# Score products of the gated levels: the moving operand cut from all 128 tokens of a chunk to the 64 that query

## The chip, the cores and the metric

The kernel runs on one NeuronCore of a Trainium2 chip, in one launch. The metric is the device time of that launch in microseconds (us), lower is better. In the profile PE is the matrix engine (TensorE) that streams a moving operand through stationary weights, PEld is the same engine's weight loads, DVE is VectorE, ACT is ScalarE, POOL is GpSimd, and SP is the engine whose queue issues the DMAs.

## The reference, cut to what matters

One layer of a hybrid decoder runs over a prompt of 2048 tokens and over 8 samples of 8 tokens, all float32. The layer has four retention heads and four gated heads (HGRN2) side by side, then an output projection and a squared-ReLU MLP.

```python
# gated heads: f = lb + (1 - lb) * sigmoid(x W_f), k = 1 - f, log_g = log f, dk = dv = 128
b = jnp.cumsum(gb, axis=2)                                   # within a chunk, per key dimension
diff = b[:, :, :, None, :] - b[:, :, None, :, :]
decay = jnp.exp(jnp.where(causal[:, :, None], diff, -jnp.inf))
A = jnp.einsum('bhtd,bhsd,bhtsd->bhts', qb, kb, decay)       # score of query t with key s
o = jnp.einsum('bhts,bhsv->bhtv', A, vb) + jnp.einsum('bhtd,bhdv->bhtv', qb * jnp.exp(b), S)
S_new = S * jnp.exp(b_last)[..., None] + jnp.einsum('bhsd,bhsv->bhdv', kb * jnp.exp(b_last - b), vb)
```

The score matrix `A` of a gated head has a decay for each of the 128 key dimensions, so it is not one matrix product. The change lies in how the kernel makes `A`.

## The kernel before, in words

**Groups and heads.** The 2112 tokens are three groups with 640, 768 and 704 columns (`GROUPS`); the last holds the 64 sample tokens ahead of 640 prompt tokens. A group's prompt tokens are chunks of 128: 5, 6 and 5 of them, 16 in all. `mix` goes through the heads p = 0 to 3 of a group. For each it issues six projections, a value product (L744 to L751) and, interleaved with these, the score and state work of one retention and one gated head. After the three groups come the MLPs, which end the program and which the change does not touch.

**Operands.** The projections run as split float32: weights and activations are each a rounded part and a remainder (`hi`, `lo`), and `proj` (L344) issues three products for each block and half of the columns, 320, 384 or 352 columns at a time. Score products run in plain float32 straight from the slabs, `[128, 768]` tiles of SBUF. The profile shows each of these as two matmul instructions, each with a weight load of its own.

**Levels of a gated head.** The 128x128 scores of a chunk are made level by level. At level w the chunk falls into blocks of 2w tokens. With the log decay measured from the middle of a block, `decayed` (L908, L909) fills a slab `qk`: keys times decay in the first half of each block, queries times decay in the second half. One product over the 128 key dimensions then gives the scores of all pairs (key in a first half, query in the second half of the same block). The levels are w = 64, 32, 16, 8, 4 and 2:

- 64 and 32 are made by `corners` (L978): one matmul for each block, w columns of weights and w moving columns.
- 16, 8 and 4 (blocks of 32 to 8 tokens) are made by `kept`: one matmul for each chunk with the whole `qk` of the chunk as both weights and moving operand (L921), then one masked copy for each half of the group's chunks (`copy_predicated`, L922). It moves into the score tile `AT` what the mask `msk[:, i]` selects. That mask is nonzero only for a key in a first half and a query in the second half of the same block.
- 2 is made by column sums over products (`quad`, L512, L513, L1010). The diagonal and the neighbouring pairs go the same way (`own`, L942; `next_to`, L965).

For the sample tokens, level 4 alone has `kept` with sg = 2: one 128x128 product (L915) and a masked copy into `ATs` (L916).

**Order of the work.** `at`, `later` and `tick` form an agenda: one tick passes with each block of projection matmuls, and the work of a head falls due so many ticks after its start. What each engine finally does in which order is decided when the program is built: a scheduler places the instructions by an estimate of their durations, except for those held by `keep_in_program_order`. An engine runs its own list in order and waits on semaphores for the others.

**Names used below.** `mm` are PSUM tiles of 512 columns from a pool of four, `po` those in which a head's outputs add up (L1101 and L1103; L784 and L787 for the samples), `AT`/`ATs` the gated scores, `qm` the sample queries that POOL copies (L780), `ret_s` and `hg_s` the sample states that SP loads (L772).

Of the kernel before, what the change touches and what calls it, by code (L numbers as in the profile page):

```python
# [15 lines left out]
P = 128  # L16
# [5 lines left out]
NS = NSEQ * SLEN  # L22
# [11 lines left out]
LEVELS = (64, 32, 16, 8, 4, 2)  # L34
NLV = len(LEVELS) + 2
# [167 lines left out]
class Kernel:  # L203
# [659 lines left out]
    def mixer(self, g, p, b, t0):  # L863


        nc, T, n0 = self.nc, g.T, g.ns
        con, msk = self.con, self.msk
        n = g.n // C
        q, k, f = b["q"], b["k"], b["f"]
        rq, rk = b["rq"], b["rk"]  # L870
        cols = [slice(n0 + C * c, n0 + C * (c + 1)) for c in range(n)]
# [38 lines left out]

        def kept(i, qk, sg):

            if sg == 2:
                ps = self.mm(P)
                nc.tensor.matmul(ps, qk[:, :P], qk[:, :P], start=True, stop=True)  # L915
                nc.vector.copy_predicated(self.ATs, msk[:, NLV + i], ps)  # L916
                return
            seg, m = g.segs[sg], len(g.segs[sg])
            ps = self.mm(m * P)
            for j, c in enumerate(seg):  # L920
                nc.tensor.matmul(ps[:, j * P:(j + 1) * P], qk[:, cols[c]], qk[:, cols[c]], start=True, stop=True)  # L921
            nc.vector.copy_predicated(self.AT[sg][:, :m], msk[:, i].unsqueeze(1).to_broadcast([P, m, P]),  # L922
                                      ps.rearrange("p (c t) -> p c t", t=P))


        def own_products():
# [86 lines left out]
        def level(i, sg):  # L1013
            w = LEVELS[i]
            if w == 2:
                quad(sg)
            elif w >= 32:
                corners(w, sg)
            else:
                kept(i, x["qk", w], sg)  # L1020
# [113 lines left out]
        for i, w in enumerate(LEVELS):  # L1134
            t = 6 + step * i
# [12 lines left out]
        t = 6 + step * len(LEVELS)  # L1148
# [680 lines left out]
```

## Time and profile before

| | |
|---|---|
| median of 3 runs | 2497.9 us (2497.9 to 2498.38) |
| profiled execution, own time | 2499.3 us |
| its span | 2497.5 us |
| PE busy / PEld busy | 2483.4 / 2465.2 us |
| DVE / ACT / POOL busy | 1883.1 / 1246.5 / 371.2 us |
| granted PE clock | 0.999 |
| L921, PE busy | 54.4 us, 384 instructions |
| L922, DVE busy | 39.0 us, 72 instructions |

The span runs from the first to the last instruction of the core; the execution's own time is 1.8 us more. A busy time is a union: where two matmuls overlap in the records, the time is counted once. The duration in a row for one matmul or weight load is from its start to its end, and several are under way at a time, so what one costs a full PE is the distance from its start to the next one's start, not its duration. The mixing stage with the levels lies between about 50 and 1120 us.

### The profile page before, as it was taken

What the parts mean: (1) busy time and instruction counts of PE and PEld (TensorE: products, weight loads), DVE (VectorE), ACT (ScalarE), POOL (GpSimd) and SP (SyncE); (2) the same over time, 40 slices, a digit from 0 to 9 for tenths busy, and PEclk for the clock granted to TensorE, in tenths of its full rate; (3) what the DMA queues carried; (4) which work ended last, traced back from release to release, by engine and by line L of the source; (5) the groups of instructions that cost most, each with busy time, mean ns of one, the idle gap of its engine ahead of it and who ended that gap; (6) DMA issues with size and microseconds to landing.
All of it is one profiled execution on the core that took longest, in us unless ns stands there. A gap on an engine that the chain in (4) does not pass through costs nothing.

```text
span 2497.5 us, 41452 instructions
## 1 busy us (share of the span) xinstructions
PE 2483.4 (99%) x16536; PEld 2465.2 (99%) x16536; DVE 1883.1 (75%) x2453; ACT 1246.5 (50%) x1674; POOL 371.2 (15%) x312
## 2 busy tenths in 40 slices
PE   9999999999999999999999999999999999999998
PEld 9999999999999999999999999999999999999998
DVE  7666866667685766686875899776699878778987
ACT  6665653444464444453644554544454436445544
POOL 5223304324411442340000000000000000000000
PEclk9999999999999999999999999999999999999999
DMA  7454575465566665868866856576675545867552
GB/s 264 170 183 172 206 252 180 161 228 186 189 205 244 216 217 197 265 210 257 283 222 214 284 196 214 176 237 222 201 264 177 188 151 192 282 195 246 195 188 89
DMA packets 191655, 525.67 MB, mean 210 GB/s; under 512 B 20963, under 2 KB 62435, under 8 KB 191462
## 3 DMA queue, kind: packets, MB, share of 16 engines
q1 hardware_dynamic: 191318, 523.01, 61.9%
q8 instruction: 130, 2.13, 0.3%
q14 instruction: 63, 0.52, 0.1%
q10 hardware_dynamic: 144, 0.02, 0.0%
HBM read 389.51 MB, written 132.39 MB: 209 GB/s over the span
## 4 chain that ended last, share of the span: by engine, by line
PE 97%; DVE 1%; ACT 1%; DMA 0%; issue 0%; SPq 0%; DVEq 0%; ACTq 0%
PE pj L344 29%; PE pf L1212 26%; PE pj L1212 25%; PE pjv L751 8%; PE mm L921 2%; PE po L1101 1%; PE mm L1109 1%; PE po L1103 1%; PE mm L978 1%; PE mm L513 1%; PE mm L512 1%; PE mm L1035 1%; PE mm L853 1%; PE po L787 1%; DMA slab<-x 0%
## 5 line engine op out<-in xcount | busy, mean ns | idle before, releaser
L273 ACT CAST hi<-raw 128x1024 fp32r<-128x1024 f32 x392 | 411.8, 1050 | 612.7 <-PE pf L1212 258.0
L344 PE MATMUL pj<-slab,hi 128*128 128x320 f32 (+2 forms) x3072 | 660.7, 328 | 2.9 <-DVE slab L650 1.3
L1212 PE MATMUL pf<-slab,hi 128*128 128x320 f32 (+2 forms) x2768 | 658.4, 321 | 0.0
L1212 PE MATMUL pj<-slab,hi 128*128 128x352 f32 (+2 forms) x2608 | 621.3, 322 | 0.0
L287 DVE TENSOR_TENSOR lo<-raw,hi 128x1024 fp32r<-128x1024 f32 x392 | 486.2, 1241 | 113.2 <-ACT hi L273 107.8
L344 PEld LDWEIGHTS pj<-slab,hi 128*128 128x128 f32 x3072 | 508.2, 188 | 5.7 <-DVE slab L650 1.6
L1212 PEld LDWEIGHTS pf<-slab,hi 128*128 128x128 f32 x2768 | 481.2, 188 | 0.0
L1212 PEld LDWEIGHTS pj<-slab,hi 128*128 128x128 f32 x2608 | 453.7, 188 | 0.1
L1212 PE MATMUL pf<-slab,lo 128*128 128x320 f32 (+2 forms) x1384 | 444.7, 321 | 0.0
L1212 PE MATMUL pj<-slab,lo 128*128 128x352 f32 (+2 forms) x1304 | 419.5, 322 | 0.0
L344 PE MATMUL pj<-slab,lo 128*128 128x320 f32 (+2 forms) x1536 | 379.0, 328 | 0.6 <-DVE lo L287 0.6
L344 PEld LDWEIGHTS pj<-slab,lo 128*128 128x128 f32 x1536 | 263.3, 188 | 1.5 <-DVE lo L287 1.1
L1212 PEld LDWEIGHTS pf<-slab,lo 128*128 128x128 f32 x1384 | 259.6, 188 | 0.0
L1212 PEld LDWEIGHTS pj<-slab,lo 128*128 128x128 f32 x1304 | 244.6, 188 | 0.0
L751 PE MATMUL pjv<-hi,slab 128*128 128x256 f32 (+1 forms) x1056 | 199.4, 285 | 0.0
L1303 ACT CAST slab<-slab 128x640 fp32r<-128x640 f32 (+2 forms) x192 | 145.4, 778 | 64.2 <-DVE slab L1314 51.7
L1307 DVE TENSOR_TENSOR slab<-slab 128x640 fp32r<-128x640 f32 (+2 forms) x192 | 167.3, 887 | 8.5 <-PE pj L1212 2.8
L751 PEld LDWEIGHTS pjv<-hi,slab 128*128 128x128 f32 (+1 forms) x1056 | 166.3, 190 | 1.4
L751 PE MATMUL pjv<-lo,slab 128*128 128x256 f32 (+1 forms) x528 | 149.2, 283 | 0.0
L902 ACT ACTIVATE slab<-slab 128x640 f32<-128x640 f32 (+2 forms) x72 | 56.3, 782 | 154.2 <-POOL slab L898 154.0
L751 PEld LDWEIGHTS pjv<-lo,slab 128*128 128x128 f32 (+1 forms) x528 | 100.3, 190 | 0.0
L1557 DVE TENSOR_TENSOR slab<-pf,slab 128x640 f32<-128x640 f32 (+2 forms) x88 | 77.7, 888 | 29.5 <-PE pf L1212 29.1
(222 smaller groups left out, 3012.4 us busy)
## 6 DMA issues: line engine op xcount, KB each, us to landing
raw<-w SPq DMA_DIRECT2D x264, 512.0 KB, 4.2
slab<-u SPq DMA_DIRECT2D x32, 384.0 KB, 4.6
u<-ld SPq DMA_DIRECT2D x30, 384.0 KB, 4.5
slab<-u SPq DMA_DIRECT2D x32, 352.0 KB, 4.5
u<-ld SPq DMA_DIRECT2D x30, 352.0 KB, 3.7
slab<-u SPq DMA_DIRECT2D x32, 320.0 KB, 5.0
u<-ld SPq DMA_DIRECT2D x30, 320.0 KB, 4.0
ld<-x SPq DMA_DIRECT2D x16, 384.0 KB, 3.8
```

What stands on the lines that cost most here:

```text
L273: self.nc.scalar.copy(hi, raw)
L287: self.nc.vector.tensor_tensor(out=lo, in0=self.second.pop(j), in1=hi.bitcast(F32), op=ALU.subtract)
L344: self.nc.tensor.matmul(pj[:, i, :T2], w, a[:, c0:c1], start=j == 0 and q == 0, stop=j == n - 1 and q == 2)
L512: self.nc.tensor.matmul(ps, self.ones_r, hi, start=True, stop=False)
L513: self.nc.tensor.matmul(ps, self.ones_r, lo, start=False, stop=True)
L751: nc.tensor.matmul(pj[:m, i * 256:(i + 1) * 256], a[:, s:s + m], ww, start=kb == 0 and q == 0, stop=m == C and kb == KB - 1 and q == 2, sk ...
L902: nc.scalar.activation(x["dd", w][:, a:T], x["dd", w][:, a:T], AF.Exp)
L921: nc.tensor.matmul(ps[:, j * P:(j + 1) * P], qk[:, cols[c]], qk[:, cols[c]], start=True, stop=True)
L1212: self.nc.tensor.matmul(*a, **k)
L1303: self.nc.scalar.copy(hi[:, :g.T], B[name][:, :g.T])
L1307: self.nc.vector.tensor_tensor(out=lo[:, :g.T], in0=B[name][:, :g.T], in1=hi.bitcast(F32)[:, :g.T], op=ALU.subtract)
L1557: nc.vector.tensor_tensor(out=r, in0=ps, in1=r, op=ALU.add)
```

## The change

In `kept` the moving operand is cut to the second halves of the blocks. The view `second` takes, of 128 columns, the w columns of the second half of each block: 64 columns, in runs of w = 16, 8 or 4 float32 values. The weights stay the whole chunk. The PSUM tile, the target in `AT` and the mask are cut to the same columns, so a masked copy goes over 64 columns of each chunk where it went over 128. For the samples the moving operand is the 32 columns of second halves among the 64 sample tokens, and the copy goes over these 32.

```diff
         def kept(i, qk, sg):
 
+            w = LEVELS[i]
+            second = lambda t: t.rearrange("p (n h m) -> p n h m", h=2, m=w)[:, :, 1]
             if sg == 2:
-                ps = self.mm(P)
-                nc.tensor.matmul(ps, qk[:, :P], qk[:, :P], start=True, stop=True)
-                nc.vector.copy_predicated(self.ATs, msk[:, NLV + i], ps)
+                ps = self.mm(NS // 2).rearrange("p (n m) -> p n m", m=w)
+                nc.tensor.matmul(ps, qk[:, :P], second(qk[:, :NS]), start=True, stop=True)
+                nc.vector.copy_predicated(second(self.ATs[:, :NS]), second(msk[:, NLV + i, :NS]), ps)
                 return
             seg, m = g.segs[sg], len(g.segs[sg])
-            ps = self.mm(m * P)
+            ps = self.mm(m * P // 2).rearrange("p (c n m) -> p c n m", c=m, m=w)
             for j, c in enumerate(seg):
-                nc.tensor.matmul(ps[:, j * P:(j + 1) * P], qk[:, cols[c]], qk[:, cols[c]], start=True, stop=True)
-            nc.vector.copy_predicated(self.AT[sg][:, :m], msk[:, i].unsqueeze(1).to_broadcast([P, m, P]),
-                                      ps.rearrange("p (c t) -> p c t", t=P))
+                nc.tensor.matmul(ps[:, j], qk[:, cols[c]], second(qk[:, cols[c]]), start=True, stop=True)
+            nc.vector.copy_predicated(self.AT[sg][:, :m].rearrange("p c (n h m) -> p c n h m", h=2, m=w)[:, :, :, 1],
+                                      second(msk[:, i]).unsqueeze(1).to_broadcast([P, m, P // (2 * w), w]), ps)
```

The scheduler places a few instructions differently because of it. Lines behind `kept` stand two lines further down in the changed kernel (L921 is L923, L922 is L924).

On PE the first place is the sample part of group 2, here head 1. L784 and L787 are the sample outputs, L810 the transposes of the sample keys, L838 the sample state products, L344 the projections around them. Before:

```order
L853 MATMUL mm<-con,slab 128x128 x3
L344 MATMUL pj<-slab,hi 128x352 x4
L344 MATMUL pj<-slab,lo 128x352 x2
L784 MATMUL po<-slab 128x128
L787 MATMUL po<-slab,ld 128x128 x8
L344 MATMUL pj<-slab,hi 128x352 x4
L344 MATMUL pj<-slab,lo 128x352 x2
L344 MATMUL pj<-slab,hi 128x352 x4
L344 MATMUL pj<-slab,lo 128x352 x2
L344 MATMUL pj<-slab,hi 128x352 x2
L810 MATMUL mm<-con,slab 96x128 x2
L838 MATMUL mm<-slab 128x512 x2
```

The same place on PE in the changed kernel:

```order
L853 MATMUL mm<-con,slab 128x128 x3
L344 MATMUL pj<-slab,hi 128x352 x2
L784 MATMUL po<-slab 128x128
L787 MATMUL po<-slab,ld 128x128 x8
L344 MATMUL pj<-slab,hi 128x352 x2
L344 MATMUL pj<-slab,lo 128x352 x2
L344 MATMUL pj<-slab,hi 128x352 x4
L344 MATMUL pj<-slab,lo 128x352 x2
L344 MATMUL pj<-slab,hi 128x352 x4
L344 MATMUL pj<-slab,lo 128x352 x2
L344 MATMUL pj<-slab,hi 128x352 x4
L810 MATMUL mm<-con,slab 96x128 x2
```

The retention samples' outputs (L784, L787) come four projection matmuls earlier, and the key transposes (L810) two later; L838 still follows L810 directly, and the gated samples' outputs, behind these rows, keep their distance of seven projection matmuls from L810.

On SP, in the same head, the loads around the sample states of the retention head; `w17hi` and `w17lo` are stored parts of a weight block. Before:

```order
L796 DMA ld<-slab 32x256 x2
L772 DMA ld<-ret_s 128x4x128
L256 DMA hi<-w17hi 128x1024
L256 DMA lo<-w17lo 128x1024
L772 DMA ld<-ret_s 128x4x128
```

And in the changed kernel:

```order
L796 DMA ld<-slab 32x256 x2
L256 DMA hi<-w17hi 128x1024
L256 DMA lo<-w17lo 128x1024
L772 DMA ld<-ret_s 128x4x128 x2
L1251 DMA sd11S_10121<-raw 128x1024
```

The first of the two state loads now stands behind the two weight loads.

On DVE, in head 0 of group 0, the masked copies of levels 8 and 4 between other work; L908 and L909 fill the `qk` slab of level 2, AT_173 and AT_174 are the two halves of `AT`. Before:

```order
L922 COPY_PREDICATED AT_173<-msk,mm 128x256
L908 TENSOR_TENSOR slab<-slab 128x160x2
L909 TENSOR_TENSOR slab<-slab 128x160x2
L922 COPY_PREDICATED AT_174<-msk,mm 128x384
L989 TENSOR_TENSOR slab<-slab 128x640
```

And in the changed kernel:

```order
L924 COPY_PREDICATED AT_173<-msk,mm 128x16x8
L908 TENSOR_TENSOR slab<-slab 128x160x2
L924 COPY_PREDICATED AT_174<-msk,mm 128x24x8
L909 TENSOR_TENSOR slab<-slab 128x160x2
L991 TENSOR_TENSOR slab<-slab 128x640
```

The second masked copy of level 8 has moved ahead of L909. Elsewhere PE shows differences of the same kind in head 3 of group 0 (column sums L512 and L513 up to eight projection matmuls later, outputs and states by one to four) and in head 3 of group 2. The products of `corners` and of `kept` keep their places in all heads, and POOL's list is unchanged.

## Prediction

> **What bounds the kernel now.** I read the page's busy times and its chain first, to see which engine sets the end; then what PE waits for; then, by line, the instructions that the change touches; then PE's two record streams in order of time, to see what one of these instructions costs.
>
> The page's span, its busy times, and the chain that ended last by engine:
>
> ```profile
> span 2497.5 us, 41452 instructions
> PE 2483.4 (99%) x16536; PEld 2465.2 (99%) x16536; DVE 1883.1 (75%) x2453; ACT 1246.5 (50%) x1674; POOL 371.2 (15%) x312
> PE 97%; DVE 1%; ACT 1%; DMA 0%; issue 0%; SPq 0%; DVEq 0%; ACTq 0%
> ```
>
> PE is the bound: 97% of the chain, and all but 14.1 us of the 2497.5 us span busy. So a microsecond off PE's stream is a microsecond off the time, and one off another engine is worth only what PE waits for it. The waits of PE come to seven rows, 5.6 us in all; the first and the last:
>
> ```profile
> PE pj L344 <- DVE slab L650: 1.3, 1, 1.3
> ...
> PE po L784 <- DVE slab L814: 0.2, 1, 0.2
> ```
>
> No row is of L921 or of a product that reads AT. But PE and PEld are both busy 99%, and this is one engine with two streams, loads of weights and matmuls. Which of the two sets the pace decides what fewer moving columns are worth. The products of the levels, by line and form:
>
> ```profile
> L921 PE MATMUL mm<-slab 128*128 128x128 f32 x384 | 54.4, 274 | 0.0
> L921 PEld LDWEIGHTS mm<-slab 128*128 128x128 f32 x384 | 51.9, 191 | 0.1
> L915 PE MATMUL mm<-slab 128*128 128x128 f32 x8 | 1.5, 272 | 0.0
> L978 PE MATMUL mm<-slab 128*64 128x64 f32 x128 | 12.6, 231 | 0.0
> L978 PEld LDWEIGHTS mm<-slab 128*64 128x64 f32 x128 | 9.2, 137 | 3.4 <-issue 0.8
> L978 PEld LDWEIGHTS mm<-slab 128*32 128x32 f32 x256 | 9.9, 112 | 5.3 <-issue 3.5 <-PE mm L1027 0.9 <-ACT slab L351 0.6
> ```
>
> 16 chunks, 4 heads, 3 levels and 2 instructions for each product make the 384, with 8 for the samples: 392 passes are touched. The mean time of one load goes 112, 137, 191 ns for 32, 64 and 128 columns of weights: some 0.8 ns for each column on top of a fixed part of some 87 ns. The weights keep their 128 columns.
>
> **What one pass costs.** The weight loads in order of time (start, length, count), at a run of four and at a run of six loads of L921, each up to the next load of a projection:
>
> ```profile
> 288.40 0.56 PEld L921 LDWEIGHTS mm<-slab 128*128 128x128 f32 x4
> 288.88 0.59 PEld L344 LDWEIGHTS pj<-slab,hi 128*128 128x128 f32 x4
> ...
> 216.16 0.78 PEld L921 LDWEIGHTS mm<-slab 128*128 128x128 f32 x6
> 216.86 0.19 PEld L344 LDWEIGHTS pj<-slab,hi 128*128 128x128 f32 x1
> ```
>
> Four loads take 0.48 us from start to start and six 0.70 us; the two more cost 0.22 us, so a pass costs 0.11 us. Load and matmul both have 128 columns here, and the two views cannot say which of them takes the 0.11. This place can, where the array has just been emptied, behind blocks of level 64 (L978, loads of 64 columns):
>
> ```profile
> 409.20 0.42 PEld L978 LDWEIGHTS mm<-slab 128*64 128x64 f32 x6
> 409.69 0.19 PEld L751 LDWEIGHTS pjv<-hi,slab 128*128 128x128 f32 x1
> 409.80 0.19 PEld L751 LDWEIGHTS pjv<-lo,slab 128*128 128x128 f32 x1
> ...
> 409.69 0.39 PE L751 MATMUL pjv<-hi,slab 128*128 128x256 f32 x1
> ```
>
> The matmul at 409.69 has nothing ahead of it but its own weight load, which starts with it. The next load starts when the first set of weights has gone into use, 0.11 us later. No earlier matmul can be what that load waits for: a load of 128 columns by itself takes the 0.11 us. And the six 64-column loads take (0.42 - 0.137)/5 = 0.057 us each from start to start, half of it, with 64 moving columns. So load and matmul cost alike per column, the load of one pass runs beside the matmul of the pass before, and the longer of the two is paid.
>
> The Trainium skill bears on this in its page "TensorE: Matmul & The Clock Gate", section "LDWEIGHTS (loading the stationary operand)", and speaks against the change: a load takes its columns of weights divided by 1.2 in ns, whatever the rows. By that rule, as an estimate, 128 columns take 107 ns and a pass could not fall below that. The emptied array's 0.11 us agrees.
>
> **The change part by part.**
>
> *The 392 passes.* Each matmul would take about 0.057 us by itself instead of 0.11, but the load of the next pass (128 columns, 0.11 us) still stands between it and the next matmul. A run of m chunks paid 2m times 0.11 us; afterwards it pays 2m loads of 0.11 us, and the projection's load behind the run also takes 0.11. What is late next is the weight load, at once. I take 0 us. The views resolve 10 ns, so the difference of six and four loads is good to 5 ns a pass; that bounds a gain, 392 x 0.005 = 2.0 us. The moving operand is now read in runs of 16, 8 or 4 values with equal gaps; no matmul of before does that. The nearest rows are DVE's masked copies, with contiguous and with every-second-column targets:
>
> ```profile
> L922 DVE COPY_PREDICATED AT<-msk,mm 128x384 f32<-128x384 uint8 x48 | 28.6, 595 | 15.1 <-PE mm L921 8.9 <-issue 4.0 <-ACT slab L902 1.6
> L922 DVE COPY_PREDICATED AT<-msk,mm 128x256 f32<-128x256 uint8 x24 | 10.6, 443 | 7.1 <-PE mm L921 3.4 <-ACT slab L902 1.8 <-issue 1.8
> L1010 DVE COPY_PREDICATED AT<-msk,mm 128x64 f32<-128x64 uint8 x128 | 22.8, 325 | 10.7 <-PE mm L513 10.7
> L965 DVE COPY_PREDICATED AT<-msk,mm 128x192 f32<-128x192 uint8 x16 | 9.3, 633 | 3.2 <-PE mm L513 3.2
> ```
>
> Contiguous, one more column costs (595 - 443)/128 = 1.2 ns; with a step of two, (633 - 325)/128 = 2.4 ns, twice as much. If PE's reading slowed by the same factor, a pass would stream 2 x 0.057 = 0.114 us, 4 ns over the load: 392 x 0.004 = 1.6 us slower. So this term is 0, from -2.0 to +1.6 us. The place in the array (rows, columns of weights) stays, so no array has to be emptied that was not.
>
> *The 72 masked copies.* They go over 128 or 192 columns instead of 256 or 384. At the contiguous price the 24 small ones cost 443 - 128 x 1.2 = 289 ns and the 48 large ones 595 - 192 x 1.2 = 365 ns: 24.5 us for all against 39.2 now. At the price with a step of two, 325 + 64 x 2.4 = 479 and 633 ns: 41.9 us. DVE's sum therefore goes down by 15 us or up by 3; runs of 4 to 16 lie nearer to contiguous, so I expect less. On the path it is 0 either way: DVE is at 75%, PE waits nowhere for L922, and the next reader of AT (L1101) comes many ticks later. If that cover were gone, a slower copy would cost PE 40 ns a place.
>
> *What the scheduler moved.* In group 2 the retention samples' outputs come four projection matmuls (0.65 us) earlier. They need POOL's query copies and the states that SP loads. The rows of head 1 (POOL, then SP, then PE), and the landing times of all L772 loads:
>
> ```profile
> 924.09 0.77 POOL L780 COPY slab<-slab 128x32 f32<-128x32 f32 x2
> ...
> 933.03 0.38 SPq L256 DMA_DIRECT2D lo<-w17lo  x1
> 933.46 0.44 SPq L772 DMA_DIRECT2D ld<-ret_s  x1
> 944.40 1.32 SPq L772 DMA_DIRECT2D ld<-hg_s  x2
> ...
> 949.00 1.95 PE L787 MATMUL po<-slab,ld 128*128 128x128 f32 x16
> 955.26 0.49 PE L784 MATMUL po<-ATs,slab 128*128 128x128 f32 x2 [0.23 <-DVE slab L814]
> ...
> DMA to landing us min/median/max: 2.9/4.1/6.6
> ```
>
> The copies end at 924.9. The first state load now stands behind the two loads of w17, so both are issued at about 933.5 to 934.5 and land by 941.1 at the slowest. PE wants them at 949.0, now 948.3: 7 us to spare. Behind the moved loads on SP stand stores of weight sums and the next weights, moved by less than 1 us. The gated samples need the second states, landed by 945.7 + 6.6 = 952.3 against 955.3. They also show the one short wait of this part, 0.23 us, for DVE's L814 behind the key transposes L810. Both move two projection matmuls later together, so that wait stays. In head 3 of group 0 column sums of the gate move by at most eight projection matmuls, 1.2 us, and PE reads what follows from them only in the last part of the output projection. I take 0. A reordering can free a wait, at most the seven rows' few tenths here, 0.8 us, or make one: two of the longest kind seen (1.3 us), 2.6 us. DVE's row swap moves L909, whose slab `quad` multiplies several ticks later: 0.
>
> **Sum.** 0 + 0 + 0 us, from -2.8 to +4.2. The profiled execution took 2499.3 us (span 2497.5 and 1.8 around it), 1.4 us over the median of the runs, so the same sum on the median gives 2497.9 us, from 2495.1 to 2502.1. Something under 0.2%, 5.0 us, is what a measurement of this kernel can tell from no change, and the sum lies inside it.
>
> **The rivals.**
>
> *The matmul sets the pace, not the load* (faster). Then 392 passes fall from 0.11 to 0.057 us: 392 x 0.053 = 20.8 us, and the time is 2477.1 us. For it: PE's busy time is above PEld's in the rows of L921 and L978, and no run of short matmuls on 128-column weights exists in the trace, so the case was never seen at work. Against it: the 0.11 us of a lone load at 409.69. It would need loads that overlap each other, and every load here waits for the one before. The section "Back-to-back issue gap" of the same page of the Trainium skill has a gap set by the moving columns alone, 134 cycles for 128 and about 60 for 64, which is this rival; the page calls that the isolated gap. Chance 0.11.
>
> *The broken moving operand is read slowly* (slower). A pass of 64 columns costs nothing until it takes 0.11 us, which is 1.7 ns a column; the price in matmuls now is 0.057/64 = 0.9 ns. At DVE's 2.4 ns a column it would take 0.154 us, 0.044 us over the load: 392 x 0.044 = 17.2 us, 2515.1 us. For it: DVE does pay double for gaps. Against: DVE's rows have gaps after every value, here 4 to 16 values stand together, and a factor of two would still hide behind the load. In the Trainium skill the page "SBUF — State Buffer" says that SBUF reads stay at full rate within lines of 16 bytes, four float32 values; that would leave this rival nothing, and no run here shows it. Chance 0.09.
>
> *A new wait in the sample part* would stay within the sum's +2.6 us, so it is in the forecast's range and not a case of its own.
>
> **How the numbers follow.** The forecast, load-bound passes, has 0.80: the load's price is read from an array with nothing else in it, and the rest of the sum is small. It gives 2497.9 us. Its bounds are 2495.1 to 2502.1, and with the 0.5 us by which the runs of before spread, 2494.6 to 2502.6. The two rivals lie outside and are the 0.20 left out. Faster by over 0.2%: 0.11. Slower: 0.09. Within: 0.80.
>
> **What would show it.** Right: in the changed profile the row of L923 on PE has 128x64 and shorter single matmuls, but from the first load of a run of six to the projection's load behind it there are still 0.70 us, and PEld's busy time on the line stays at some 52 us. DVE's row for L924 is below 39 us while PE's waits stay under 8 us in all. Wrong towards faster: that run of six takes 0.4 us. Wrong towards slower: it takes over 0.75 us, most at level 4 with its runs of four; or PE shows waits of 1 us and more at L784 or L787.

## The result, and the profile after

The changed kernel takes 2495.28 us (median of 21 runs, 2494.6 to 2497.38) against 2497.9 us before (21 runs, 2497.21 to 2499.61): ratio 0.9989, 95% interval [0.9983, 0.9995]. That is 2.6 us, 0.11%, faster. It lies inside the range and inside 0.2%, but the interval does not hold 1, and the forecast was no change: there is a small gain that the sum did not contain. The profiled execution took 2495.74 us.

The page's span, busy times and chain, after:

```profile
span 2493.9 us, 41450 instructions
PE 2480.4 (99%) x16536; PEld 2463.2 (99%) x16536; DVE 1876.4 (75%) x2453; ACT 1246.3 (50%) x1674; POOL 372.5 (15%) x312
PE 98%; DVE 1%; ACT 0%; DMA 0%; issue 0%; SPq 0%; DVEq 0%
```

PE is still the bound. The groups by line and form, after (a count, busy us, mean ns of one, then idle us ahead of them):

```profile
L923 PEld LDWEIGHTS mm<-slab 128*128 128x128 f32 x384 | 51.9, 191 | 0.1
L923 PE MATMUL mm<-slab 128*128 128x64 f32 x384 | 50.6, 264 | 0.0
L924 DVE COPY_PREDICATED AT<-msk,mm 128x192 f32<-128x192 uint8 x48 | 17.5, 366 | 20.0 <-PE mm L923 13.6 <-issue 4.2 <-ACT slab L902 1.5
```

The matmul has 64 moving columns now and its record is 10 ns shorter, but the loads are busy 51.9 us, to the digit as before. The loads in order of time, at the two places that the prediction read, after:

```profile
216.38 0.78 PEld L923 LDWEIGHTS mm<-slab 128*128 128x128 f32 x6
217.09 0.59 PEld L344 LDWEIGHTS pj<-slab,hi 128*128 128x128 f32 x4
...
288.53 0.56 PEld L923 LDWEIGHTS mm<-slab 128*128 128x128 f32 x4
289.01 0.59 PEld L344 LDWEIGHTS pj<-slab,hi 128*128 128x128 f32 x4
```

0.71 us for six and 0.48 for four, against 0.70 and 0.48 before. Over all runs of loads on the line, from the second load of a run to the second one behind it, the median is 442 ns for the 24 runs of four and 667 ns for the 48 runs of six, in both kernels. The passes did not become cheaper, apart from 12 runs that come below. So where do 2.6 us come from?

I took the start times of the 14,288 matmuls of the projections, value products and MLPs, which stand in the same sequence in all kernels here, and compared each with its twin in a second profile of before (e1 below), counted from about 25 us on. Negative is ahead, in us:

| kernel | end of group 1 (787 us) | head 1 of group 2 (988) | end of mixing (1197) | 2040 | 2211 |
|---|---|---|---|---|---|
| before | -0.07 | -0.07 | -0.13 | -0.12 | +1.58 |
| after | -0.49 | -1.39 | -2.43 | -2.43 | -2.43 |
| after again (e2) | -0.50 | -1.40 | -2.43 | -2.43 | -0.72 |
| after, third (e9) | -0.46 | -1.36 | -2.47 | -2.46 | -2.46 |
| e5, narrow matmul | -0.50 | -0.44 | -1.10 | -1.10 | +0.61 |
| e6, narrow copy | +0.17 | +0.03 | -0.32 | -0.32 | -0.32 |
| e7, woven | -3.99 | -5.66 | -3.60 | -3.60 | -3.60 |
| e8, woven but last head | -4.04 | -5.71 | -7.20 | -7.20 | -5.50 |

The step of 1.7 us between 2080 and 2200 us comes and goes between executions of one and the same kernel, in a stretch of MLP that the change does not touch, so it is no part of the change. What belongs to it is the 2.4 us of the mixing stage: 0.4 to 0.5 us in groups 0 and 1, and 1.9 us in group 2, the only group with a sample part.

**Where the 1.9 us lie.** The wait rows of PE's matmuls fell only from 5.6 to 5.3 us; 0.3 us of that is the row of L344 behind L650 that the prediction showed, 1.3 before and 1.0 after. Most of the missing time is in rows that the prediction did not read: those of the weight loads, of the sample outputs above all. By line and form, before:

```profile
L784 PEld LDWEIGHTS po<-slab 128*128 128x128 f32 x8 | 1.3, 189 | 0.5 <-ACT slab L855 0.3 <-issue 0.3
L784 PEld LDWEIGHTS po<-ATs,slab 128*128 128x128 f32 x8 | 1.2, 189 | 0.7 <-DVE slab L814 0.7
L513 PEld LDWEIGHTS mm<-slab,ones_r 128*128 128x128 f32 x112 | 21.0, 188 | 0.4 <-DVE slab L352 0.4
```

The last columns are idle time ahead of the loads, 1.6 us in all. The same groups, after:

```profile
L784 PEld LDWEIGHTS po<-slab 128*128 128x128 f32 x8 | 1.4, 188 | 0.0
L784 PEld LDWEIGHTS po<-ATs,slab 128*128 128x128 f32 x8 | 1.4, 189 | 0.0
L513 PEld LDWEIGHTS mm<-slab,ones_r 128*128 128x128 f32 x112 | 21.0, 188 | 0.0
```

All gone. From the load ahead to the load named, in ns, in order of time:

| place | before | before again | after |
|---|---|---|---|
| L784, retention, head 1 | 473 | 467 | no wait |
| L784, gated, head 1 | 715 | 712 | 164 |
| L784, gated, head 2 | 398 | 400 | no wait |
| L513, head 3 | 566 | 531 | no wait |
| L344 behind L853, head 3 | 1695 | 1694 | 1415 |
| L784, retention, head 3 | 445 | 444 | no wait |

With about 160 ns for a load that waits for nothing, the six places give 2.1 us; a new 331 ns ahead of L1111 in head 3 takes 0.2 back. That is 1.9 us net; with the four shorter runs of group 2 (0.2 us, below) the rows add up to slightly more than the positions show.

The two engines at the gated output of head 1. Before, DVE's L814 (the last to write what L784 reads) and the load that waits for it:

```profile
954.79 0.42 DVE L814 TENSOR_TENSOR slab<-mm,slab 32x256 fp32r<-32x256 f32 x1
955.25 0.30 PEld L784 LDWEIGHTS po<-ATs,slab 128*128 128x128 f32 x2 [0.52 <-DVE slab L814]
```

After:

```profile
954.22 0.42 DVE L814 TENSOR_TENSOR slab<-mm,slab 32x256 fp32r<-32x256 f32 x1
954.69 0.35 PEld L784 LDWEIGHTS po<-ATs,slab 128*128 128x128 f32 x2
```

DVE reaches L814 0.57 us earlier, and the load starts 0.56 us earlier without a wait. DVE's rows ahead of it show two reasons. Before:

```profile
946.97 0.95 DVE L672 SCALAR_TENSOR_TENSOR slab<-slab,vec 128x704 f32<-128x704 f32 x1 [1.33 <-ACT slab L364]
950.17 0.29 DVE L1010 COPY_PREDICATED AT<-msk,mm 128x64 f32<-128x64 uint8 x1
950.31 0.23 DVE L1008 COPY_PREDICATED ATs<-msk,mm 128x32 f32<-128x32 uint8 x1
950.40 1.31 DVE L1010 COPY_PREDICATED AT<-msk,mm 128x64 f32<-128x64 uint8 x8
```

After:

```profile
946.70 0.95 DVE L672 SCALAR_TENSOR_TENSOR slab<-slab,vec 128x704 f32<-128x704 f32 x1 [0.64 <-ACT slab L364]
949.92 1.02 DVE L1012 COPY_PREDICATED AT<-msk,mm 128x64 f32<-128x64 uint8 x6
```

L672, where DVE waits for ACT, starts 0.27 us earlier. And of the ten masked copies of `quad` that stood behind that wait, four (three into `AT`, one into `ATs`) now stand ahead of it, in time in which DVE waits anyway; that is the other 0.30 us. The trace does not show why the scheduler places them there; e5 and e6 below show which half of the change each of the two parts comes with.

**Where the 0.5 us lie.** Of the 72 runs on L923, 12 are about 50 ns shorter than before, 0.6 us in all. They are the runs with the transposes of L853 directly behind them, one in each head: eight in groups 0 and 1, which give 0.39 of the 0.4 to 0.5 us there, and four in group 2. One such place, the last load of the run and the first of the transposes, before and after:

```profile
62.06 0.19 PEld L921 LDWEIGHTS mm<-slab 128*128 128x128 f32 x1
62.17 0.14 PEld L853 LDWEIGHTS mm<-con,slab 128*128 128x128 f32 x1
```

```profile
62.46 0.19 PEld L923 LDWEIGHTS mm<-slab 128*128 128x128 f32 x1
62.52 0.20 PEld L853 LDWEIGHTS mm<-con,slab 128*128 128x128 f32 x1
```

The transpose's load follows 0.06 us after the product's instead of 0.11. With 64 moving columns the product itself takes 0.057 us. If the longer of matmul and next load is paid, the load of a transpose cannot need more than that, while the load of another product or of a projection needs 0.11.

### The profile page after: what moved, and what is told of

Read it like the earlier page. It is cut to its first block, busy times and chain, and to the rows that moved or that the text cites. A ratio compares the mean times of both kernels' runs of the same rounds, so it can differ in the third digit from the quotient of the medians.

```text
span 2493.9 us, 41450 instructions
## 1 busy us (share of the span) xinstructions
PE 2480.4 (99%) x16536; PEld 2463.2 (99%) x16536; DVE 1876.4 (75%) x2453; ACT 1246.3 (50%) x1674; POOL 372.5 (15%) x312
## 4 chain that ended last, share of the span: by engine, by line
PE 98%; DVE 1%; ACT 0%; DMA 0%; issue 0%; SPq 0%; DVEq 0%
PE pj L344 29%; PE pf L1214 26%; PE pj L1214 25%; PE pjv L751 8%; PE mm L923 2%; PE mm L1111 1%; PE po L1103 1%; PE po L1105 1%; PE mm L980 1%; PE mm L513 1%; PE mm L512 1%; PE po L787 1%; PE mm L1037 1%; PE mm L853 1%; DMA slab<-x 0%; ACT slab L549 0%
## 5 line engine op out<-in xcount | busy, mean ns | idle before, releaser
L344 PE MATMUL pj<-slab,hi 128*128 128x320 f32 (+2 forms) x3072 | 661.6, 328 | 2.9 <-DVE slab L650 1.0
L344 PEld LDWEIGHTS pj<-slab,hi 128*128 128x128 f32 x3072 | 508.1, 188 | 5.5 <-DVE slab L650 1.3
L344 PE MATMUL pj<-slab,lo 128*128 128x320 f32 (+2 forms) x1536 | 379.5, 327 | 0.6 <-DVE lo L287 0.6
L344 PEld LDWEIGHTS pj<-slab,lo 128*128 128x128 f32 x1536 | 263.7, 188 | 1.8 <-DVE lo L287 1.1
```

What stands on the lines that cost most here:

```text
L344: self.nc.tensor.matmul(pj[:, i, :T2], w, a[:, c0:c1], start=j == 0 and q == 0, stop=j == n - 1 and q == 2)
```

## The experiments

**Both kernels again.** e1 is before and e2 is after, unchanged, to tell what a second execution moves.

> The kernel before, unchanged, for a second profile. It tells which parts of the 3.6 us between the first two profiled spans repeat. In those two profiles, counted on the projection matmuls, the changed kernel loses 0.57 us in the first 25 us, gains 0.45 us spread over groups 0 and 1, 1.85 us in four steps in the sample part of group 2, and 1.7 us at an even 2 ns a matmul between 2075 and 2210 us, where both run the same code. My theory (passes unchanged, waits around the samples gone): the loss at the start and the even stretch are not the change's and differ again between two runs of the same kernel by up to 2 us; the waits of group 2 (0.32 and 0.55 us at L784 in head 1, 0.24 us in head 2, 0.4 us at L513 and 1.7 us behind L853 in head 3) come again within 0.1 us each. Rival (the gain is a general one, all over the program): the even stretch comes again as it was.

> The changed kernel, unchanged, for a second profile. Theory: the sample part of group 2 is again some 1.9 us shorter than in the kernel before, twelve runs of level products (those with transposes L853 right behind them) are again some 50 ns shorter, 0.6 us in all, and all other runs cost what they did (0.44 us from the second load of a run of four to the second load behind it, 0.67 us for six). Rival: runs are shorter by 7 ns a pass, 2.6 us over 392 passes.

They took 2497.31 and 2496.5 us, one execution each. The waits of before came back within 35 ns, and those of after stayed away; the 12 shorter runs came back too. The stretch from 2080 to 2200 us did not repeat. It holds 747 matmuls in before and 755 in e1, by the windows of before and of e1 (columns: busy time and count of PE, PEld, DVE, ACT, POOL, then clock, DMA share, GB/s):

```profile
2080.00:2200.00 120.00, 120.00 (x747) 119.92 (x745) 94.61 (x111) 63.02 (x77) 0.00 (x0) 1.00 0.73 243
```

```profile
2080.00:2200.00 120.00, 120.00 (x755) 119.92 (x755) 95.39 (x111) 62.86 (x76) 0.00 (x0) 1.00 0.73 242
```

PE is busy throughout and its clock is full in both, so nothing in these rows names the cause; after has 756 here and e2 has 746. A single profile therefore cannot settle a difference of 1.7 us on its end time, and the positions at the end of mixing are compared instead.

**What sets the pace of a pass.** If it is the longer of load and matmul, then making both half as long (e3) must halve the pass, and halving the load alone (e4) must not. e3 is after with the weights cut to the first 64 keys; e4 is before with weights cut so and 128 moving columns. The scores of the other 64 keys are left out in both. The lines of the matmul, against after and against before (the masked copies are cut to the same 64 rows):

```diff
+            half = P // 2
-                nc.tensor.matmul(ps[:, j], qk[:, cols[c]], second(qk[:, cols[c]]), start=True, stop=True)
+                nc.tensor.matmul(ps[:half, j], qk[:, cols[c].start:cols[c].start + half], second(qk[:, cols[c]]), start=True, stop=True)
```

```diff
+            half = P // 2
-                nc.tensor.matmul(ps[:, j * P:(j + 1) * P], qk[:, cols[c]], qk[:, cols[c]], start=True, stop=True)
+                nc.tensor.matmul(ps[:half, j * P:(j + 1) * P], qk[:, cols[c].start:cols[c].start + half], qk[:, cols[c]], start=True, stop=True)
```

> The changed kernel with the weights of the prompt products cut as well, to the first 64 columns of the chunk, so that load and matmul both have 64; the scores of the other 64 keys are left out. The instructions stand in the same order on all engines as in the changed kernel. Theory (the load sets the pace of a pass): inside a run each pass falls from 0.111 to 0.058 us; a run of 2m passes saves 2m - 1 of them, since the projection's load behind it stays at 128 columns: (24 x 3 + 48 x 5) x 0.053 = 16.5 us, 2478.8 us. If a change of the number of weight columns makes the array run empty, 72 runs lose up to 0.2 us each at both ends and most of that is given back. Rival (a float32 pass has a floor of 0.11 us for another reason): no change from the changed kernel, 2495 us.

> The kernel before with only the weights of the prompt products cut to 64 columns, moving operand still 128; the scores of the other 64 keys are left out, and the instructions stand in the order of the kernel before. Theory (the longer of load and matmul is paid): the matmul's 0.108 us takes the load's place, a pass falls by 2 to 3 ns, 0.8 us in all: 2497 us. Rival (load and matmul add up in part): 5 us and more faster.

e3 took 2498.45 us, 1.0002 [0.9992, 1.0011]; e4 2519.76 us, 1.0082 [1.0067, 1.0098]. Inside a run both did as the theory says: 58 ns a pass in e3 and 109 ns in e4, where the matmul took the load's place as the longer part. The times did not follow (2478.8 and 2497 us were expected), because of the ends of a run. e3, loads in order of time:

```profile
216.28 0.34 PEld L344 LDWEIGHTS pj<-slab,lo 128*128 128x128 f32 x2
216.81 0.42 PEld L924 LDWEIGHTS mm<-slab 128*64 128x64 f32 x6 [0.19 <-issue]
217.30 0.59 PEld L344 LDWEIGHTS pj<-slab,hi 128*128 128x128 f32 x4
```

e4:

```profile
218.34 0.33 PEld L344 LDWEIGHTS pj<-slab,lo 128*128 128x128 f32 x2
218.86 0.41 PEld L924 LDWEIGHTS mm<-slab 128*64 128x64 f32 x4 [0.19 <-issue]
219.44 0.44 PEld L344 LDWEIGHTS pj<-slab,hi 128*128 128x128 f32 x3 [0.17 <-issue]
```

Between loads of 128 and of 64 columns PE stops: the first load of a run comes 380 ns behind the load ahead in e3, where 147 are normal, and some 0.1 to 0.2 us are lost again behind the run. In e4, where the passes cost what they did, the runs, each from the load ahead of it to the second load behind it, take 23 us more than in before, 0.32 us for each of 72. Shorter waits, above all in the last head (714 ns behind L853 instead of 1695), give some of it back; at the end of mixing e4 is 20.7 us behind. In e3 the same sum over the runs is 3.4 us more than in before: the ends eat the 384 x 0.053 = 20 us that the short passes save, and somewhat more. The caveat in e3's expectation decided the result: it allowed for most of the gain to be given back, and all of it was. e4's expectation did not price the emptying, and missed.

**Which half of the change frees the waits.** e5 keeps the 64-column products for the prompt tokens but copies 128 columns, reading the product twice (the sample product as before); e6 keeps the 128-column products and copies 64 columns. The main lines of each, against after:

```diff
-            nc.vector.copy_predicated(self.AT[sg][:, :m].rearrange("p c (n h m) -> p c n h m", h=2, m=w)[:, :, :, 1],
-                                      second(msk[:, i]).unsqueeze(1).to_broadcast([P, m, P // (2 * w), w]), ps)
+            nc.vector.copy_predicated(self.AT[sg][:, :m].rearrange("p c (n h m) -> p c n h m", h=2, m=w),
+                                      msk[:, i].rearrange("p (n h m) -> p n h m", h=2, m=w).unsqueeze(1).to_broadcast([P, m, P // (2 * w), 2, w]),
+                                      ps.unsqueeze(3).to_broadcast([P, m, P // (2 * w), 2, w]))
```

```diff
-                nc.tensor.matmul(ps[:, j], qk[:, cols[c]], second(qk[:, cols[c]]), start=True, stop=True)
+                nc.tensor.matmul(ps[:, j * P:(j + 1) * P], qk[:, cols[c]], qk[:, cols[c]], start=True, stop=True)
-                                      second(msk[:, i]).unsqueeze(1).to_broadcast([P, m, P // (2 * w), w]), ps)
+                                      second(msk[:, i]).unsqueeze(1).to_broadcast([P, m, P // (2 * w), w]),
+                                      ps.rearrange("p (c n h m) -> p c n h m", c=m, h=2, m=w)[:, :, :, 1])
```

> Only the prompt products are cut to 64 moving columns; the masked copies still go over 128 columns of each chunk (the product is read twice, the mask keeps the second halves), and the sample product is as before. In heads 0 to 2 of group 2 the instructions stand almost as in the changed kernel, and the first sample output (L784 in the kernel before) waits for DVE and PE instead of ACT. Theory A (the waits of the sample part went because of the order, in which the sample outputs get other PSUM buffers): the two waits of head 1 (0.32 and 0.55 us) and the one of head 2 (0.24 us) are gone or mostly gone, the transposes behind level products bring 0.6 us, and the mixing stage is some 2 us shorter than in the kernel before, 2495.5 to 2496 us. Theory B (they went because the shorter masked copies relieve DVE): the waits stay, and only the 0.6 us remain, 2497.3 us.

> Only the masked copies are cut to the second halves; the products keep their 128 moving columns. In heads 0 to 2 of group 2 the instructions stand as in the kernel before, and the first sample output waits for ACT as there; DVE's copies take 0.36 us instead of 0.59. Theory A (order): the waits at the sample outputs of heads 1 and 2 stay, no pass is shorter, 2497 to 2498 us. Theory B (DVE relieved): the waits are gone, some 1.1 us in heads 1 and 2 and up to 0.7 us in head 3, 2496 us. No theory has a shorter run of level products here.

e5 took 2496.3 us (0.9993 [0.9984, 1.0002]), e6 2497.26 us (0.9995 [0.9986, 1.0004]). Neither interval excludes 1, so the positions in the table are what can be read: by the end of mixing e5 had gained 1.1 us, e6 0.3, after 2.4. Neither the matmul half nor the copy half alone is the cause, as each of the two theories would have it. The 12 shorter runs are there in e5 and not in e6, so 0.6 of e5's 1.1 us are theirs. e5, by line and form, then two of DVE's rows in time:

```profile
L784 PEld LDWEIGHTS po<-slab 128*128 128x128 f32 x8 | 1.4, 188 | 0.0
L784 PEld LDWEIGHTS po<-ATs,slab 128*128 128x128 f32 x8 | 1.3, 188 | 0.9 <-DVE slab L814 0.9
L924 DVE COPY_PREDICATED AT<-msk,mm 128x384 f32<-128x384 uint8 x48 | 28.5, 594 | 20.3 <-PE mm L923 14.5 <-issue 3.7 <-ACT slab L902 1.5
...
947.27 0.95 DVE L672 SCALAR_TENSOR_TENSOR slab<-slab,vec 128x704 f32<-128x704 f32 x1 [1.39 <-ACT slab L364]
950.51 1.01 DVE L1013 COPY_PREDICATED AT<-msk,mm 128x64 f32<-128x64 uint8 x6
```

e6:

```profile
L784 PEld LDWEIGHTS po<-slab 128*128 128x128 f32 x8 | 1.3, 189 | 0.6 <-issue 0.4
L784 PEld LDWEIGHTS po<-ATs,slab 128*128 128x128 f32 x8 | 1.3, 188 | 0.7 <-DVE slab L814 0.5 <-DVE ld L842 0.2
L924 DVE COPY_PREDICATED AT<-msk,mm 128x192 f32<-128x192 uint8 x48 | 17.5, 364 | 16.4 <-PE mm L923 9.4 <-issue 4.5 <-ACT slab L902 1.7
...
946.73 0.95 DVE L672 SCALAR_TENSOR_TENSOR slab<-slab,vec 128x704 f32<-128x704 f32 x1 [1.19 <-ACT slab L364]
950.16 1.31 DVE L1013 COPY_PREDICATED AT<-msk,mm 128x64 f32<-128x64 uint8 x8
```

In e5 the scheduler also puts the retention output early, and its wait is gone. But PE then comes to the gated output 0.56 us earlier than before while DVE's L814 is only 0.18 us earlier (954.61), and the wait there grows from 0.5 to 0.9 us. That wait is the 0.95 us by which e5 is behind after at head 1 of group 2. In e6 the copies are short, but the early order is missing: in head 1 the gated output's wait stays (709 ns from load to load), the retention output's shrinks to 330 ns, and head 3 has longer waits (603 and 377 ns). The wait of head 2 is gone in both.

DVE's rows show the two parts of its lead apart. e5 has the four `quad` copies ahead of the wait for ACT (six are left behind L672) but reaches L672 late, at 947.27; e6 reaches it early, at 946.73, but has the copies behind it, as before. Of the three only after has both. So the moved copies are not owed to the shorter copies of L924, which are long in e5; they come with the narrow product. The two halves give 1.1 + 0.3 = 1.4 us by themselves, and the last 1.0 us only together. Each kernel has an order of its own from the scheduler, so these runs show which waits go with which half, and not a change of one instruction's place.

**Using the short load of a transpose.** If a transpose directly behind a 64-column product saves 0.05 us, more of them can stand there. e7 puts one behind each product of level 16 (transposes of the retention keys) and of level 4 (gated keys), 128 in all, and makes level 4 after level 2, where its keys are ready (main lines, against after):

```diff
             for j, c in enumerate(seg):
                 nc.tensor.matmul(ps[:, j], qk[:, cols[c]], second(qk[:, cols[c]]), start=True, stop=True)
+                if turned:
+                    nc.tensor.transpose(pt[:, j * P:(j + 1) * P], src[:, cols[c]], self.ident)
...
-            t = 6 + step * i
+            t = 6 + step * {2: 4, 4: 5}.get(w, i)
```

> The changed kernel with the 128 transposes of a head's keys (weight loads of 0.055 us, matmuls of 0.108) issued one by one between the level products: those of the retention keys behind the chunks of level 16, those of the gated keys behind the chunks of level 4, for which level 4 comes after level 2. Theory (a pass costs the longer of its own matmul and the next weight load): each of 128 products of 64 columns is then followed by a load of 0.055 us and costs 0.053 us less, where in the changed kernel 12 are: 116 x 0.053 = 6.1 us, 2489.2 us; if the waits of the sample part come back with the new order, up to 1.9 us less is gained, 2491 us. Rival (a product of two float32 passes costs 0.22 us whatever follows): 2495.3 us, or slower by what the new order costs.

e7 took 2494.89 us, 0.9986 [0.9977, 0.9995], where 2489.2 to 2491 were expected: hardly better than after. The loads in order of time show the mechanism at work:

```profile
136.19 0.33 PEld L928 LDWEIGHTS mm<-slab 128*128 128x128 f32 x2
136.40 0.20 PEld L930 LDWEIGHTS mm<-con,slab 128*128 128x128 f32 x1
136.51 0.31 PEld L928 LDWEIGHTS mm<-slab 128*128 128x128 f32 x2
136.68 0.20 PEld L930 LDWEIGHTS mm<-con,slab 128*128 128x128 f32 x1
```

From one transpose (L930) to the next there are 0.28 us for the two matmuls of a product and a transpose, where three passes at 0.11 would be 0.33. Up to head 1 of group 2 the kernel was 4.3 us ahead of after. At the end of mixing 1.2 us of this are left; the loss lies in head 3, where the moved level comes too late. PE waits there, and then runs at a lower clock, in the trace's record at half for 3.4 us from 1117.5 on (rows of PE in time, then the window around it, columns as above; its clock of 0.76 is a mean):

```profile
1116.67 0.41 PE L930 MATMUL mm<-con,slab 128*128 128x128 f32 x2 [1.76 <-DVE slab L1088]
1117.38 1.44 PE L344 MATMUL pj<-slab,hi 128*128 128x352 f32 x4 [0.30 <-DVE slab L650]
1118.61 0.79 PE L344 MATMUL pj<-slab,lo 128*128 128x352 f32 x2
1119.20 0.79 PE L344 MATMUL pj<-slab,hi 128*128 128x352 f32 x2
```

```profile
1116.00:1119.00 3.00, 2.03 (x8) 1.82 (x9) 3.00 (x10) 1.58 (x2) 0.00 (x0) 0.76 0.24 73
```

e8 weaves the same way except the gated keys and level 4 of that one head, which stay as in after. e9 is after on the same chip. The main lines of e8, against e7:

```diff
+        woven = not (n0 and p == H - 1)
-            elif w == 4 and sg < 2:
+            elif w == 4 and sg < 2 and woven:
```

> The woven kernel, except that in head 3 of group 2 level 4 and the transposes of the gated keys stay apart, as in the changed kernel (there the woven kernel waited 1.8 us for DVE and then ran about 1.5 us at half clock). Theory (the longer of matmul and next load is paid, waits come on top): up to head 2 of group 2 the mixing stage is as in the woven kernel, 4.3 us ahead of the changed kernel, and head 3 costs what it costs there: 2491 us, 4 us under the changed kernel. Rival (the wait in head 3 moves with the new order and stays): 2493 us and more.

> The changed kernel, unchanged, timed on the same chip for comparison with the woven one. Both theories: 2495 to 2497 us, and in a third profile again 2.4 us off the mixing stage.

e8 took 2492.13 us (2490.8 to 2492.76), 0.9975 [0.9965, 0.9985] against before; e9 2494.72 us (2494.5 to 2495.07), 0.9986 [0.9977, 0.9995]. e8's time lies between the 2491 us of its theory and the 2493 of its rival. e8's loads of the woven transposes, by line and form:

```profile
L930 PEld LDWEIGHTS mm<-con,slab 128*128 128x128 f32 x123 | 24.2, 196 | 0.0
```

The woven kernel beats both by runs that do not overlap: 5.8 us under before, 2.6 under after. Its waits at L784 are down to 0.1 us, and at the end of mixing it is 4.7 us ahead of e9, of the 6.1 us that e7's expectation counted for the shorter passes; the stretch at 2080 us gave 1.7 of it back in its profile.

## Why the prediction was right in its main step and wrong in its sum

- **The load sets the pace: right.** Six loads still take 0.71 us, PEld still 51.9 us on the line. e3 and e4 show the rule directly: 58 ns with both at 64 columns, 109 with 64 columns of weights and 128 moving. The rule of the Trainium skill, page "TensorE: Matmul & The Clock Gate", section "LDWEIGHTS (loading the stationary operand)", that a load takes its columns over 1.2 in ns, agrees: 107 ns by the page, 111 measured. The row at 409.69 did not prove it alone: in the records the L978 matmuls ahead of it end, as modelled, only at 409.76, so it does not show an empty array. e3 and e4 do not need that place.
- **The rival "The matmul sets the pace" fell** by the same rows: 667 ns for a run of six in both kernels.
- **The broken moving operand costs nothing: right**, as far as it can be seen. All that a pass of 64 columns in runs of 4 to 16 values needs hides under 0.11 us, and in e3, where nothing hides it, it is 58 ns, the contiguous price.
- **The masked copies cost the contiguous price: right.** 366 ns where 365 were worked out for the large ones, and 17.5 + 7.0 = 24.5 us for all 72.
- **The term of the passes missed a gain.** That "the projection's load behind the run also takes 0.11" holds for 60 of 72 runs. Behind 12 stand transposes, whose load is short, so there the matmul was the longer part and its cut counted: 0.6 us. A row of before had hinted at it, the loads of the transposes with a mean of 141 ns where those of L921 have 191:

```profile
L853 PEld LDWEIGHTS mm<-con,slab 128*128 128x128 f32 x128 | 16.7, 141 | 0.8
```

- **The term of the scheduler's moves was read wrong: this is the step that failed.** It was put at 0 with at most 0.8 us to gain, from "the seven rows' few tenths": the waits of PE's matmul stream. A wait of a weight load stands on the other stream. What it called "the one short wait of this part, 0.23 us" was the 0.52 us wait of its load seen from the matmul; the retention output ahead had one of 0.3 us that PE's rows did not have at all. In all 2.1 us were freed, and 1.9 net, more than twice the 0.8 us that the term allowed. The time still lies inside the range by luck: the 2.0 us that the passes were given for the resolution of the views covered what the waits gained. And the signs of a right forecast named under "What would show it" all came true, for none of them looked at the idle time ahead of weight loads.
- **"Both move two projection matmuls later together, so that wait stays": wrong.** PE and DVE do not move together: DVE came 0.57 us earlier through its own list, 0.27 us because it reached L672 earlier and 0.30 because four copies moved ahead of the wait there. DVE's 75% hid that it is late at just this place.

What stays open: e5 and e6 name the waits and the two parts of DVE's lead, but not each queue entry behind the 1.0 us that needs both halves, nor why the scheduler moves the copies with the narrow product; and the share of head 3 (1695 to 1415 ns behind L853, and two waits gone) was not taken apart. What moves the MLP stretch by 1.7 us from one execution to the next is unknown.

## What to carry to other kernels

In the products measured here a pass costs the longer of its own matmul and the next weight load, so fewer moving columns are worth something only where the load behind is short; put such loads there (e8) rather than cut columns alone. Read idle time on the weight loads as well as on the matmuls before saying that PE waits nowhere. When an edit shortens work of an idle engine, look for the places where PE comes just behind that engine; there even an engine at 75% is worth its microseconds.

## What the runs showed of the hardware that was not expected

- Going from 128 to 64 columns of weights and back makes PE stop, 0.32 us for a run in e4, though the record of each load is shorter (136 ns where 128 columns have 191).
- A transpose's load, of the same 128x128 float32 shape, seems to take at most about half of a product's: it follows a 64-column product after 0.06 us, where another load follows after 0.11. This is read from the distances (62.52 against 62.46, and e7's 0.28 us for three passes) by the rule that the longer is paid; no run measured such loads by themselves, and e8's row of them, with a mean of 196 ns, shows that the length of the record does not tell it.
- After the 1.8 us pause in e7 the granted clock was 0.76 over 3 us (half for 3.4 us, where e8's expectation took 1.5), and projection matmuls came 0.295 us apart (two in 0.59 us, from 1118.61 on) where 0.16 is usual. The Trainium skill, page "TensorE: Matmul & The Clock Gate", section "What's actually happening", has the clock halved after an idle window of about 3.4 us; in this profile one wait of 1.8 us, with another 0.3 us behind it, came ahead of the halving, while the wait of 1.3 us in before left the clock full (all three as the matmul rows have them). Of e7's 11 executions 8 list a mean clock of 0.998, those of after all 0.999, so it may not have happened in every one.
